# Four edits to a Mamba and attention encoder step: another order of PSUM banks, an earlier split of one weight tile, moved transposes, and a state update in fp32r

## The chip, the cores and the metric

The kernel runs on one core of a Trainium2 chip. The metric is the device time of one execution in microseconds; the figure for the kernel before is the median of three runs, 2209.36 us (2208.69 to 2213.75). Every instruction of the program is in the trace of one profiled execution.

## The reference

Two requests go through one network in one step: a prompt of 512 frames and a sample of 32 frames, which share all weights. Both are kept side by side as 544 columns of a matrix with 1024 rows. The layers are, in order:

```
for i in (0, 1):                                   # D_MODEL 1024, D_FF 2816, everything float32
    if i == 1: k_new, v_new = norm(x) @ w_k, norm(x) @ w_v          # 4 heads of 64
    x += 0.5 * swiglu(norm(x))                                       # FFN 2i
    x += mamba2(norm(x)) if i == 0 else stick_breaking_attention(norm(x), k, v)
    x += 0.5 * swiglu(norm(x))                                       # FFN 2i+1
    x += sigmoid(norm(x) @ w_gate) * (p[i] @ w_proj)                 # per-layer inputs
return norm(x), states, new keys and values
```

Mamba's recurrence is evaluated by chunks, 32 heads in 4 groups of 8. For a chunk with its inputs `x_c`, `B_c`, `C_c` and the summed decay `a_cs`:

```
y         = (C_c B_c^T * decay) x_c + (C_c state) * exp(a_cs)
new_state = state * exp(a_cs[-1]) + B_c^T (exp(a_cs[-1] - a_cs) * x_c)       # the state update
```

The new state of each group is 128 x 512 (state size by heads times head size). The outputs include the final states, the new keys and values, and the convolution's last rows.

## The kernel before

**Products.** A float32 product is made from three products of fp32r parts. An operand is split into a high part (`hi`, a copy by ScalarE or GpSimd that rounds to fp32r) and a low part (`lo`, the rest, by a subtraction on VectorE or GpSimd); the sum of `hi*hi`, `hi*lo` and `lo*hi` is gathered in PSUM. Weights arrive by DMA in tiles of 128 x 1024, are split on chip into `whi` and `wlo`, and are used once. A down, gate or input product of 128 rows takes 8 blocks of 3 parts and 2 column halves of 272. A few small products run in plain float32 instead: the transposes, Mamba's per-head products and the state update, which is one matmul of 512 columns.

**Who orders the work.** In FFNs, Mamba and attention the order on TensorE, VectorE, ScalarE and GpSimd is written by a planner (`Plan`, line 67). The work is a set of chains, each of which yields requests: `T`, `S`, `V`, `G` with an estimated time for an instruction on an engine, `get` and `put` for a buffer slot, `wait` and `set` for an event, `spawn` for a new chain with a rank. `run` (line 145) takes the request that can start first by its own model; among those that could start at the same time, the lowest rank goes first. The engines then run their lists strictly in that order. Outside these three stages (the keys and values, the per-layer inputs, the end) the framework orders the instructions.

**FFN** (`Sevens`, line 579). Most of a product is made by seven products of half size instead of eight. The last four hidden blocks of the FFN go into the output as four plain units `("d", 0)` to `("d", 3)`: units 0 and 1 begin and finish output tiles 0 to 3, unit 2 makes tiles 4 and 5, unit 3 tiles 6 and 7. Each finished tile is added to `x` by VectorE (`leave`, rank 9), and then the next layer's operand is made from it (`onward`, rank 2: `xh` or `nh` on ScalarE, `xl` or `nl` on VectorE, a square on ScalarE and `acc` on VectorE). `halve` (line 745, rank 10) splits a weight tile. There are three weight slots (`NW`); one lies in memory that closes with the stage, and the last three units of the list may not use it. In FFN 0 and 2 a tile of the next stage follows unit `("d", 3)` in the list; in FFN 1 and 3 it is the last.

**PSUM of FFN and its neighbours.** `banks` (line 2067) gives four pairs of banks, pair k being banks 2k and 2k+1. A counter goes round them: each `psum()` and each `roles()` moves it by one. `roles()` with the counter at k gives the FFN's roles A, B, D, X the pairs k, k+1, k+3, k+2 modulo 4. The last tiles 4, 5, 6, 7 go into A, B, D, X where the swaps of A and X between the products come out even, as they do in FFN 2 (16 of them). From FFN 1 to FFN 2 one counter, which starts at 2, serves `roles()`, then 17 calls in the per-layer inputs, then the keys, then `roles()` again.

**Keys and values** (`keys`, line 1605). Four products in the order v0, v1, k0, k1, with the norm's scale after the first. Then the two value tiles are transposed in five blocks of rows, each into a `psum()` of its own, copied to SBUF by VectorE, and stored to memory by two DMAs.

**Attention** (line 1633). Its PSUM pool has four tags: `z` (4 banks), `f` (1), `o` (1), `tr` (2). A tag gets its banks when it is first used. The first four query products go into banks in the order of `FIRSTQ`; the first one takes two `z` banks, one for each column half, and works on blocks 0 to 6 of the first half (21 matmuls), then of the second, and then on block 7.

**Mamba** (line 1110). `dense` walks through the list `MSEQ`: `i` is the six input products of a group (B, C and four x), `z` its gates, `o` its outputs; it has the lowest priority. A group's inputs lie in a slot `grp`, of which there are two. `ssd(g)` works through five chunks, four of the prompt and one of the sample (32 rows), and gives `grp` back when the last is out. For each chunk:

- `turn_x` transposes x, scales it (`xd`, VectorE) and weighs it for the state (`xw`, GpSimd).
- `turn_b` transposes B and copies it (`btok`, VectorE).
- `decay` makes `ex` on ScalarE and VectorE; `decay_ab` makes `exp` of the summed decay on ScalarE and multiplies it by C on GpSimd (`ab`, for chunks after the first).
- `state` does the matmul `btok` by `xw` and adds the old state, decayed on GpSimd.
- `output` (which waits for `ex`, `xd`, `xw`, `ab` and the state before) does the heads' products and adds the skip.

Of the kernel before, what the change touches and what calls it, by code (L numbers as in the profile page):

```python
# [9 lines left out]
P = 128  # L10
# [3 lines left out]
TS = 32  # L14
# [168 lines left out]
def v_cost(n):  # L183
    return n / 960.0 + 0.069


def _body(tc, io):
# [22 lines left out]
    with ExitStack() as ctx:  # L210
# [368 lines left out]
        class Sevens:  # L579
# [91 lines left out]
            def weights(self):  # L671
                raw, tmp = self.raw, self.tmp
                for k, u in enumerate(self.units):
# [48 lines left out]
                    if u[0] == "p" and self.opened and u[1] >= LOWER:  # L722
                        yield "spawn", self.lower(k, src, hi, lo, free), 10
                    else:
                        yield "spawn", self.halve(k, n, src, hi, lo, free), -2 if k == 0 and self.opened else 10

            def fourth(self, it):
                yield "wait", ("part", self.index[it, 2])
# [381 lines left out]
        def mamba(norm, after, ready, ahead):  # L1110
            with tc.tile_pool(name="mt", bufs=1, reuse_waits="tile") as tmp, \
# [254 lines left out]
                def decay_ab(g, c, ab):  # L1366
                    off, n = chunks[c]
                    src = off if c < 4 else SOFF
                    ct = got["C", g][:, src:src + n]
                    yield "S", s_cost(8 * n), lambda: S.activation(ab, ab, AF.Exp), "exp"  # L1370
                    yield "get", "fade"
                    fade = got["fade", g, c] = tmp.tile([P, 8, 1], F32, tag="fade", name="fade", bufs=2)
                    yield "V", 0.08, lambda: V.tensor_copy(fade, ab[:, :, n - 1:n])
                    yield "set", ("fade", g, c)
                    if c > 0:
                        yield "G", 0.06 + 8 * n * 2.28e-3, lambda: G.tensor_tensor(out=ab, in0=ab, in1=ct.unsqueeze(1).to_broadcast([P, 8, n]), op=ALU.mult)
                    yield "set", ("cd", g, c)

                def turn_x(g, c):
                    off, n = chunks[c]  # L1380
                    src = off if c < 4 else SOFF
                    xs = got["x", g]
                    yield "get", "xd"
                    yield "get", "aux"
                    px = aux()

                    def turn():
                        for t in range(4):
                            TE.transpose(px[:n, t * P:(t + 1) * P], xs[:, t, src:src + n], ident)
                    yield "T", 0.44, turn  # L1390
                    xd = got["xd", g, c] = tmp.tile([P, 8, 64], F32, tag="xd", name="xd", bufs=2)
                    yield "W", v_cost(512), lambda: V.tensor_tensor(out=xd[:n], in0=px[:n, :].rearrange("p (h d) -> p h d", d=64),
                                                                 in1=tok[:n, c, 32 + 8 * g:40 + 8 * g].unsqueeze(2).to_broadcast([n, 8, 64]), op=ALU.mult)
                    yield "put", "aux"
                    yield "set", ("xd", g, c)
                    yield "get", "xw"
                    xw = got["xw", g, c] = tmp.tile([P, 8, 64], F32, tag="xw", name="xw", bufs=2)
                    yield "G", 1.0, lambda: G.tensor_tensor(out=xw[:n], in0=xd[:n],
                                                             in1=tok[:n, c, 64 + 8 * g:72 + 8 * g].unsqueeze(2).to_broadcast([n, 8, 64]), op=ALU.mult)
                    yield "set", ("xw", g, c)  # L1400

                def turn_b(g, c):
# [3 lines left out]
                    yield "get", "aux"  # L1406
                    pb = aux()
                    yield "T", 0.11, lambda: TE.transpose(pb[:n, :P], got["B", g][:, src:src + n], ident)
                    btok = got["bt", g, c] = tmp.tile([P, P], F32, tag="btok", name="btok", bufs=1)
                    yield "W", v_cost(P), lambda: V.tensor_copy(btok[:n, :], pb[:n, :P])  # L1410
                    yield "put", "aux"
                    yield "set", ("bt", g, c)

# [10 lines left out]
                def state(g, c):  # L1424
# [4 lines left out]
                    yield "T", 0.87, lambda: TE.matmul(pst, got["bt", g, c][:n, :], got["xw", g, c][:n].rearrange("p h d -> p (h d)"), start=True, stop=True)  # L1429
                    yield "put", "xw"  # L1430
                    yield "put", "btok"
                    if c > 0:
# [23 lines left out]
                def output(g, c):  # L1456
                    off, n = chunks[c]
                    src = off if c < 4 else SOFF
                    xs = got["x", g]
                    need = [("ex", g, c), ("xd", g, c), ("xw", g, c), ("cd", g, c)]  # L1460
                    yield "wait", *need
                    if c > 0:
                        yield "wait", ("st", g, before(c))
# [141 lines left out]
        def keys(norm, psum, tmp, ring, kept, side):  # L1605
# [3 lines left out]
            for which in (1, 0):  # L1609
                for a in range(2):  # L1610
# [7 lines left out]
                    nc.scalar.dma_start(io["kv_out"][which, a], t)  # L1618
                    if which:
                        vT[a] = t  # L1620
                    else:
                        nc.gpsimd.dma_start(kept[0][:, a, :], t)
            vt = side.tile([P, 5, 256], F32, name="vtok")
            for blk in range(5):
                n = P if blk < 4 else TS
                ps = psum()
                for a in range(2):
                    TE.transpose(ps[:n, 0, a * P:(a + 1) * P], vT[a][:, blk * P:blk * P + n], ident)
                V.tensor_copy(vt[:n, blk, :], ps[:n, 0, :256])
            nc.gpsimd.dma_start(kept[1], vt[:, 0:4, :])  # L1630
            nc.gpsimd.dma_start(kept[2], vt[:TS, 4, :])

        def attention(norm, after, ready, ahead, kept):
            with ExitStack() as keep, \
# [11 lines left out]

                def bank(tag):
                    return pp.tile([P, 512], F32, tag=tag, name=tag, bufs=BANKS[tag])

                def two(tag="z"):  # L1650
                    return [bank(tag), bank(tag)]
# [674 lines left out]
```

## Time and profile before

| what | value |
|---|---|
| median of three runs | 2209.36 us |
| profiled execution, its own time | 2208.82 us |
| its span, first to last instruction | 2207.0 us |
| TensorE clock granted, mean | 0.998 |
| busy: TensorE, VectorE, ScalarE, GpSimd | 99%, 81%, 52%, 28% |

The span is what the trace covers; 1.82 us of the profiled execution lie around it. All instructions that go through the kernel's helper class carry its line, L199, so groups are told apart by the names of their tiles. In a timeline a row is: start in us, length in us, engine, line, operation, output<-inputs, shape, count, and in brackets the idle time before it and what ended that. The length of a matmul's row runs past the start of the next, since matmuls are pipelined and their ends are modelled: what a matmul costs is read from the starts of the rows.

### The profile page before, as it was taken

To read this page: it belongs to the slowest core of one execution; us is meant where nothing else is said; L and a number is where in the kernel's file an instruction comes from. 1 tells how busy PE (TensorE), PEld (TensorE's weight loads), DVE (VectorE), ACT (ScalarE), POOL (GpSimd) and SP (SyncE) were. 2 spreads that over 40 slices of the span, in tenths; PEclk is the share of its full clock that TensorE was granted. 3 is DMA by queue.
4 is the path that set the end of the run, shared out by engine and by line. 5 is a ranking of instruction groups with operands and counts; after the bars stand their busy time and mean duration, and the time that the engine had idled before them with its cause. 6 is when DMAs were issued, how large, how long until landed. Compare 5 with 4: busy or idle time off the path is not lost.

```text
span 2207.0 us, 42789 instructions
## 1 busy us (share of the span) xinstructions
PE 2182.7 (99%) x17480; PEld 2128.4 (96%) x17480; DVE 1788.0 (81%) x2460; ACT 1136.8 (52%) x1645; POOL 616.6 (28%) x610
## 2 busy tenths in 40 slices
PE   9999999999999999999999999999999999999998
PEld 9999999999999999999999999999987899999997
DVE  8988887678887689888867798888778799888866
ACT  6444534567756465445355554444456364445354
POOL 1323321254333123223210222322243223233202
PEclk9999999999999999999999999999999999999999
DMA  7686852333333276968532768685411186868422
GB/s 234 158 226 158 213 141 71 113 113 93 111 109 90 91 194 165 229 167 206 145 95 87 222 172 225 167 211 139 126 39 58 49 223 165 222 166 210 129 87 80
DMA packets 119684, 325.53 MB, mean 147 GB/s; under 512 B 15392, under 2 KB 36512, under 8 KB 119488
## 3 DMA queue, kind: packets, MB, share of 16 engines
q1 hardware_dynamic: 92192, 234.81, 32.8%
q0 software_dynamic: 24416, 82.46, 21.0%
q10 hardware_dynamic: 2880, 5.53, 0.7%
q8 instruction: 138, 2.26, 0.4%
q14 instruction: 58, 0.48, 0.1%
HBM read 316.04 MB, written 6.71 MB: 146 GB/s over the span
## 4 chain that ended last, share of the span: by engine, by line
PE 90%; DVE 5%; DMA 2%; ACT 1%; issue 1%; POOL 0%; DVEq 0%; SPq 0%; ACTq 0%; POOLq 0%
PE mm L199 79%; PE z L199 4%; PE aux L199 3%; DMA a<-in_wd 2%; PE f L199 1%; DVE wlo L199 1%; DVE x L199 1%; PE tr L199 1%; PE o L199 1%; DVE xl L199 1%; DVE s L199 1%; DMA plr<-in_p 0%; ACT xh L199 0%; DVE gu L199 0%; DVE nl L199 0%
## 5 line engine op out<-in xcount | busy, mean ns | idle before, releaser
L199 PE MATMUL mm<-xh,whi 128*128 128x272 f32 x1728 | 421.6, 293 | 1.9 <-DVE rm L199 0.9
L199 PE MATMUL mm<-xl,whi 128*128 128x272 f32 x1728 | 414.1, 288 | 0.3 <-DVE xl L199 0.3
L199 PE MATMUL mm<-xh,wlo 128*128 128x272 f32 x1728 | 413.2, 288 | 0.0
L199 PEld LDWEIGHTS mm<-xh,whi 128*128 128x128 f32 x1728 | 293.0, 188 | 11.8 <-issue 9.7
L199 PEld LDWEIGHTS mm<-xl,whi 128*128 128x128 f32 x1728 | 292.5, 188 | 0.5 <-DVE xl L199 0.5
L199 PEld LDWEIGHTS mm<-xh,wlo 128*128 128x128 f32 x1728 | 292.8, 188 | 0.0
L199 PE MATMUL mm<-xfh,whi 128*128 128x272 f32 x936 | 270.0, 288 | 0.0
L199 PE MATMUL mm<-xfh,wlo 128*128 128x272 f32 x936 | 269.9, 288 | 0.0
L199 PE MATMUL mm<-xfl,whi 128*128 128x272 f32 x936 | 269.7, 288 | 0.0
L199 DVE TENSOR_TENSOR wlo<-wraw,whi 128x1024 fp32r<-128x1024 f32 (+3 forms) x179 | 219.9, 1230 | 52.4 <-ACT whi L199 43.1
L199 ACT ACTIVATE whi<-wraw 128x1024 fp32r<-128x1024 f32 (+3 forms) x145 | 147.5, 1020 | 194.6 <-PE mm L199 137.8
L199 ACT ACTIVATE whi<-s 128x1024 fp32r<-128x1024 f32 (+1 forms) x126 | 122.2, 970 | 207.1 <-PE mm L199 99.7
L199 ACT ACTIVATE whi<-a 128x1024 fp32r<-128x1024 f32 (+1 forms) x127 | 125.4, 987 | 159.4 <-PE mm L199 107.9
L199 DVE TENSOR_TENSOR wlo<-a,whi 128x1024 fp32r<-128x1024 f32 (+1 forms) x146 | 168.4, 1154 | 30.7 <-ACT whi L199 25.9
L199 PE MATMUL mm<-h4h,whi 128*128 128x272 f32 x688 | 178.2, 289 | 3.4 <-DVE x L199 3.4
L199 PE MATMUL mm<-h4h,wlo 128*128 128x272 f32 x688 | 177.7, 289 | 1.2 <-DVE wlo L199 1.2
L199 PE MATMUL mm<-h4l,whi 128*128 128x272 f32 x688 | 177.4, 288 | 0.0
L199 PEld LDWEIGHTS mm<-xfl,whi 128*128 128x128 f32 x936 | 176.1, 188 | 0.0
L199 PEld LDWEIGHTS mm<-xfh,wlo 128*128 128x128 f32 x936 | 176.1, 188 | 0.0
L199 PEld LDWEIGHTS mm<-xfh,whi 128*128 128x128 f32 x936 | 176.0, 188 | 0.0
L199 DVE SCALAR_TENSOR_TENSOR x<-mm,x 128x544 f32<-128x544 f32 x200 | 143.8, 719 | 37.4 <-PE mm L199 37.0
L199 DVE TENSOR_TENSOR wlo<-s,whi 128x1024 fp32r<-128x1024 f32 (+1 forms) x136 | 154.8, 1138 | 21.2 <-ACT whi L199 13.3
(378 smaller groups left out, 6027.5 us busy)
## 6 DMA issues: line engine op xcount, KB each, us to landing
a<-in_wgq SPq DMA_DIRECT2D x117, 512.0 KB, 5.7
s<-in_wgq POOLq DMA_DIRECT2D x79, 512.0 KB, 7.0
a<-in_wd SPq DMA_DIRECT2D x72, 384.0 KB, 4.3
wraw<-in_win SPq DMA_DIRECT2D x41, 512.0 KB, 3.6
s<-in_wgq SPq DMA_DIRECT2D x40, 512.0 KB, 4.7
wraw<-in_wgq SPq DMA_DIRECT2D x38, 512.0 KB, 5.0
wraw<-in_wgq POOLq DMA_DIRECT2D x38, 512.0 KB, 8.3
s<-in_wd SPq DMA_DIRECT2D x24, 384.0 KB, 4.8
```

What stands on the lines that cost most here:

```text
L199: ins = getattr(self.engine, op)(*args, **kw)
```

## The change

It has four parts.

1. **Attention's banks.** A loop at the start of attention uses each tag once, so that `o` gets its bank first, then the four of `z`, then `f` and `tr`.
2. **Last down tiles.** The split of unit `("d", 3)` runs at rank 8 instead of 10, in all four FFNs.
3. **Values.** The transposes stand between the products k0 and k1. The first four blocks share one `psum()` and one copy of 128 x 1024; the fifth has its own. Three fewer `psum()` calls are made.
4. **Mamba's state update.** `xw` and the transposed B are split into fp32r parts, and the product is made from three matmuls. The high part of `xw` is a copy on ScalarE, the low part a subtraction on VectorE; B's high part is read from PSUM by ScalarE, its low part by VectorE, where the copy was. `output` waits for the new event `xr`, which is set before the split. The multiplication of `ab` by C goes from GpSimd to VectorE.

```diff
 (Sevens.weights)
-                        yield "spawn", self.halve(k, n, src, hi, lo, free), -2 if k == 0 and self.opened else 10
+                        yield "spawn", self.halve(k, n, src, hi, lo, free), -2 if k == 0 and self.opened else 8 if u[0] == "d" and u[1] == 3 else 10
 (decay_ab)
-                        yield "G", 0.06 + 8 * n * 2.28e-3, lambda: G.tensor_tensor(out=ab, in0=ab, ...)
+                        yield "V", v_cost(8 * n), lambda: V.tensor_tensor(out=ab, in0=ab, ...)
 (turn_x)
                     yield "G", 1.0, lambda: G.tensor_tensor(out=xw[:n], in0=xd[:n], ...)
+                    yield "set", ("xr", g, c)
+                    flat = xw[:n].rearrange("p h d -> p (h d)")
+                    high = tmp.tile([P, 512], F32R, tag="xwh", name="xwh", bufs=2)
+                    yield "S", s_cost(512), lambda: S.activation(high[:n, :], flat, AF.Copy)
+                    low = tmp.tile([P, 512], F32R, tag="xwl", name="xwl", bufs=2)
+                    yield "V", v_cost(512), lambda: V.tensor_tensor(out=low[:n, :], in0=flat, in1=high[:n, :].bitcast(F32), op=ALU.subtract)
+                    got["xw", g, c] = high, low
                     yield "set", ("xw", g, c)
 (turn_b)
-                    btok = got["bt", g, c] = tmp.tile([P, P], F32, tag="btok", name="btok", bufs=1)
-                    yield "W", v_cost(P), lambda: V.tensor_copy(btok[:n, :], pb[:n, :P])
+                    high = tmp.tile([P, P], F32R, tag="btok", name="btok", bufs=1)
+                    yield "S", s_cost(P, True), lambda: S.activation(high[:n, :], pb[:n, :P], AF.Copy)
+                    low = tmp.tile([P, P], F32R, tag="btol", name="btol", bufs=1)
+                    yield "W", v_cost(P), lambda: V.tensor_tensor(out=low[:n, :], in0=pb[:n, :P], in1=high[:n, :].bitcast(F32), op=ALU.subtract)
+                    got["bt", g, c] = high, low
 (state)
-                    yield "T", 0.87, lambda: TE.matmul(pst, got["bt", g, c][:n, :], got["xw", g, c][:n]..., start=True, stop=True)
+                    def products():
+                        (bh, bl), (wh, wl) = got["bt", g, c], got["xw", g, c]
+                        for k, (b, w) in enumerate(((bh, wh), (bh, wl), (bl, wh))):
+                            TE.matmul(pst, b[:n, :], w[:n, :], start=k == 0, stop=k == 2)
+                    yield "T", 0.7, products
 (output)
-                    need = [("ex", g, c), ("xd", g, c), ("xw", g, c), ("cd", g, c)]
+                    need = [("ex", g, c), ("xd", g, c), ("xr", g, c), ("cd", g, c)]
 (keys)
-                    else:
-                        nc.gpsimd.dma_start(kept[0][:, a, :], t)
-            vt = side.tile([P, 5, 256], F32, name="vtok")
-            for blk in range(5):
-                n = P if blk < 4 else TS
-                ps = psum()
-                for a in range(2):
-                    TE.transpose(ps[:n, 0, a * P:(a + 1) * P], vT[a][:, blk * P:blk * P + n], ident)
-                V.tensor_copy(vt[:n, blk, :], ps[:n, 0, :256])
-            nc.gpsimd.dma_start(kept[1], vt[:, 0:4, :])
-            nc.gpsimd.dma_start(kept[2], vt[:TS, 4, :])
+                        continue
+                    nc.gpsimd.dma_start(kept[0][:, a, :], t)
+                    if a:
+                        continue
+                    vt = side.tile([P, 5, 256], F32, name="vtok")
+                    for blks in (range(4), range(4, 5)):
+                        n = P if blks[0] < 4 else TS
+                        ps = psum()
+                        for k, blk in enumerate(blks):
+                            for b in range(2):
+                                at = 256 * (k % 2) + b * P
+                                TE.transpose(ps[:n, k // 2, at:at + P], vT[b][:, blk * P:blk * P + n], ident)
+                        V.tensor_copy(vt[:n, blks[0]:blks[-1] + 1, :]..., ps[:n, :, :]...[:, :256 * len(blks)])
+                    nc.gpsimd.dma_start(kept[1], vt[:, 0:4, :])
+                    nc.gpsimd.dma_start(kept[2], vt[:TS, 4, :])
 (attention)
+                for tag in ("o", "z", "z", "z", "z", "f", "tr", "tr"):
+                    bank(tag)
```

More of the change, by code (lines that the diff above doesn't have):

```diff
@@ L1375, in decay_ab @@
                     if c > 0:
-                        yield "G", 0.06 + 8 * n * 2.28e-3, lambda: G.tensor_tensor(out=ab, in0=ab, in1=ct.unsqueeze(1).to_broadcast([P, 8, n]), op=ALU.mult)
+                        yield "V", v_cost(8 * n), lambda: V.tensor_tensor(out=ab, in0=ab, in1=ct.unsqueeze(1).to_broadcast([P, 8, n]), op=ALU.mult)
                     yield "set", ("cd", g, c)
@@ L1396, in turn_x @@
                     yield "get", "xw"
-                    xw = got["xw", g, c] = tmp.tile([P, 8, 64], F32, tag="xw", name="xw", bufs=2)
+                    xw = tmp.tile([P, 8, 64], F32, tag="xw", name="xw", bufs=2)
                     yield "G", 1.0, lambda: G.tensor_tensor(out=xw[:n], in0=xd[:n],
                                                              in1=tok[:n, c, 64 + 8 * g:72 + 8 * g].unsqueeze(2).to_broadcast([n, 8, 64]), op=ALU.mult)
+                    yield "set", ("xr", g, c)
[5 more added lines that the diff above has]
+                    got["xw", g, c] = high, low
                     yield "set", ("xw", g, c)
@@ L1428, in state @@
                     pst = aux()
-                    yield "T", 0.87, lambda: TE.matmul(pst, got["bt", g, c][:n, :], got["xw", g, c][:n].rearrange("p h d -> p (h d)"), start=True, stop=True)
+                    def products():
[3 more added lines that the diff above has]
+                    yield "T", 0.7, products
                     yield "put", "xw"
@@ L1620, in keys @@
                         vT[a] = t
-                    else:
-                        nc.gpsimd.dma_start(kept[0][:, a, :], t)
-            vt = side.tile([P, 5, 256], F32, name="vtok")
-            for blk in range(5):
-                n = P if blk < 4 else TS
-                ps = psum()
-                for a in range(2):
-                    TE.transpose(ps[:n, 0, a * P:(a + 1) * P], vT[a][:, blk * P:blk * P + n], ident)
-                V.tensor_copy(vt[:n, blk, :], ps[:n, 0, :256])
-            nc.gpsimd.dma_start(kept[1], vt[:, 0:4, :])
-            nc.gpsimd.dma_start(kept[2], vt[:TS, 4, :])
+                        continue
[10 more added lines that the diff above has]
+                                TE.transpose(ps[:n, k // 2, at:at + P], vT[b][:, blk * P:blk * P + n], ident)
+                        V.tensor_copy(vt[:n, blks[0]:blks[-1] + 1, :].rearrange("p k n -> p (k n)"), ps[:n, :, :].rearrange("p a n -> p (a n)")[:, :256 * len(blks)])
+                    nc.gpsimd.dma_start(kept[1], vt[:, 0:4, :])
+                    nc.gpsimd.dma_start(kept[2], vt[:TS, 4, :])
         def attention(norm, after, ready, ahead, kept):
```

## The prediction

> **What bounds the kernel now.** I read the page's busy shares first, then its chain of work that ended last.
>
> ```profile
> span 2207.0 us, 42789 instructions
> ...
> PE 2182.7 (99%) x17480; PEld 2128.4 (96%) x17480; DVE 1788.0 (81%) x2460; ACT 1136.8 (52%) x1645; POOL 616.6 (28%) x610
> ...
> PE 90%; DVE 5%; DMA 2%; ACT 1%; issue 1%; POOL 0%; DVEq 0%; SPq 0%; ACTq 0%; POOLq 0%
> ```
>
> TensorE (PE) is busy all but 24.3 us of the span, so time can only be won in two ways: by giving PE less to do, or by closing one of its few gaps. Next come two stretches in the view of busy times, an FFN's and the part of Mamba in which the scan runs. The columns are the stretch, its length, and the busy time of PE, weight loads, DVE, ACT and POOL.
>
> ```profile
> 28.00:366.00 338.00, 336.93 (x2682) 336.14 (x2681) 286.58 (x362) 155.17 (x203) 92.68 (x86) 1.00 0.66 168
> 425.00:720.00 295.00, 294.10 (x2531) 275.11 (x2530) 228.73 (x420) 199.45 (x341) 111.62 (x129) 1.00 0.35 105
> ```
>
> Mamba's PE stands idle for only 0.9 of 295 us, with DVE at 78%; the FFN's PE is idle for 1.1 us with DVE at 85%. So in Mamba it is PE's own work that counts, and 85% of DVE is a load that this kind of order has borne. Last, PE's waits, by what ended them (total us, times, longest):
>
> ```profile
> PE mm L199 <- DVE wlo L199: 1.2, 2, 0.7
> PE z L199 <- DVE x L199: 1.2, 1, 1.2
> ...
> PE mm L199 <- DVE kv L199: 0.7, 1, 0.7
> ```
>
> These four gaps are what parts 1 to 3 of the change touch. What they cost PE is read from the starts of matmuls below, since a row's length runs past the next start.
>
> **The state update: less PE work.** Two stretches of PE's timeline, around a product of 128 rows and around one of the sample's 32:
>
> ```profile
> 429.92 1.02 PE L199 MATMUL aux<-xw,btok 128*128 128x512 f32 x2
> 430.37 0.81 PE L199 MATMUL mm<-xh,whi 128*128 128x272 f32 x2
> 431.02 0.41 PE L199 MATMUL mm<-xl,whi 128*128 128x272 f32 x2
> 431.27 0.41 PE L199 MATMUL mm<-xh,wlo 128*128 128x272 f32 x2
> ...
> 486.41 1.12 PE L199 MATMUL aux<-xw,btok 32*128 32x512 f32 x2
> ...
> 487.82 0.41 PE L199 MATMUL mm<-xl,whi 128*128 128x272 f32 x2
> ```
>
> A pair of fp32r matmuls of 272 columns takes 0.25 us (431.02 to 431.27), 0.125 each. From 429.92 to 431.02 lie the state product and one such pair, so the product costs 1.10 - 0.25 = 0.85 us. With 32 rows it is 1.41 - 0.25 = 1.16, of which 0.31 must be changes of shape. There are 16 of the first (four groups, four prompt chunks) and 4 of the second. An fp32r matmul of 512 columns is in the trace among attention's logits, two at a time on 64 rows each:
>
> ```profile
> 1617.57 0.40 PE L199 MATMUL z<-kl,qq 64*128 64x512 f32 x2
> 1617.81 0.39 PE L199 MATMUL z<-kh,qq 64*128 64x512 f32 x2
> ```
>
> That is 0.24 us for 512 columns; scaling 0.125 by 512/272 gives 0.235. I take 0.235, so three cost 0.705, and I let the 0.31 of the sample's shape stay. Saved: 16 x (0.85 - 0.705) = 2.3, and 4 x (1.16 - 0.705 - 0.31) = 0.6, together **2.9 us**. Bounds: 2.1 if a matmul costs 0.24 and the sample saves nothing; 5.4 if it costs 0.85/4 = 0.213 and the 0.31 goes too.
>
> **What the state update adds elsewhere.** Durations by group:
>
> ```profile
> L199 POOL TENSOR_TENSOR ab<-ab,C 128x1024 f32<-128x1024 f32 x12 | 28.7, 2392 | 30.9 <-DVE fade L199 30.9
> L199 DVE TENSOR_TENSOR ex<-ex,cb 128x1024 f32<-128x1024 f32 x16 | 19.6, 1227 | 3.5 <-ACT ex L199 3.5
> ...
> L199 DVE TENSOR_TENSOR qq<-qT,qq 128x512 fp32r<-128x512 f32 x7 | 5.6, 800 | 2.3 <-ACT qq L199 2.3
> L199 ACT ACTIVATE qq<-qT 128x512 fp32r<-128x512 f32 x6 | 3.8, 626 | 3.6 <-DVE qT L199 3.6
> ```
>
> The `ab` multiplication leaves POOL. On DVE it should take what `ex` by `cb` of the same shape takes, 1.23 us: 12 x 1.23, and some 2 us for the four of the sample, make 16.4 us. The low part of `xw` adds 20 x 0.80 = 16.0 at most, and B's low part takes the copy's place at about the same cost. DVE's load in the scan goes from 228.7 to about 261 of 295 us, 88%. ACT gets 20 x 0.63 for `xw` and some 5 us for B: about 17 on 199. All of this lies beside PE work. The split of `xw` delays only `state`, since `output` waits for `xr`; and `output`, which needs `ab`, gets it 2.39 - 1.23 = 1.16 us earlier for each chunk when DVE is free. The planner writes all of Mamba's lists anew from the changed costs. The cover that could go is the room between a group's last output and the input product that wants its `grp` slot. I put +0.2 us on the new order, with bounds from -0.9 (every idle moment closed) to +12.7 (below).
>
> **The last down tile.** DVE's, POOL's and PE's timelines near the end of FFN 1, then PE's at the end of FFN 3:
>
> ```profile
> 1133.19 1.16 POOL L199 TENSOR_SCALAR whi<-wraw 128x1024 fp32r<-128x1024 f32 x1 [8.58 <-PE mm L199]
> ...
> 1136.21 1.54 DVE L199 TENSOR_TENSOR acc<-acc,sq 128x544 f32<-128x544 f32 x2
> 1138.37 0.72 DVE L199 SCALAR_TENSOR_TENSOR x<-mm,x 128x544 f32<-128x544 f32 x1
> 1139.01 1.22 DVE L199 TENSOR_TENSOR wlo<-wraw,whi 128x1024 fp32r<-128x1024 f32 x1
> ...
> 1139.38 0.41 PE L199 MATMUL mm<-h4l,whi 128*128 128x272 f32 x2
> 1140.28 0.52 PE L199 MATMUL mm<-h4h,wlo 128*128 128x272 f32 x2 [0.48 <-DVE wlo L199]
> ```
>
> ```profile
> 2125.00 0.41 PE L199 MATMUL mm<-h4l,whi 128*128 128x272 f32 x2
> 2126.09 0.52 PE L199 MATMUL mm<-h4h,wlo 128*128 128x272 f32 x2 [0.68 <-DVE wlo L199]
> ```
>
> The high part is there at 1134.35, but DVE does the subtraction only at 1139.01, behind tile additions (rank 9) and the next norm's work (rank 2). PE could have gone on at 1139.63 and starts at 1140.28: 0.65 lost; in FFN 3, 2126.09 - 2125.25 = 0.84. At rank 8 the subtraction passes the additions, though not the rank 2 work. It needs only be done by 1139.63, and moving ahead of the addition at 1138.37 and one more is enough. The additions then come up to 1.14 us later; their next readers are PE's bank for tiles 6 and 7 and the per-layer gates, both microseconds away. FFN 0 and 2 show no wait for this tile. I take **1.4** of 1.49; bounds 0 and 1.49.
>
> **The values.** PE and DVE at the end of the keys' stage:
>
> ```profile
> 1231.72 0.82 PE L199 MATMUL mm<-ident,kv 128*128 128x128 f32 x6
> 1233.26 0.72 PE L199 MATMUL mm<-ident,kv 128*128 128x128 f32 x4 [0.72 <-DVE kv L199]
> 1234.02 0.49 PE L199 MATMUL mm<-xh,whi 128*128 128x272 f32 x2
> ...
> 1229.70 2.87 DVE L199 SCALAR_TENSOR_TENSOR xl<-x,gains,xh 128x544 fp32r<-128x544 f32 x4 [1.73 <-ACT xh L199]
> 1232.49 0.72 DVE L199 TENSOR_TENSOR kv<-mm,r 128x544 f32<-128x544 f32 x1
> ```
>
> Six transposes take 0.66 us (four of them 0.44 to 0.5), so the seventh could start at 1232.38 and starts at 1233.26. The fourth block's PSUM is the pair that k1 just filled, and DVE reads that out only after four `xl`. Moved ahead of k1, the ten transposes cost PE the same, but find v0's and the scale's pairs long free: **0.9 us** saved. What is late next: FFN 2's first operand. Its `xl` move with k1, about 1.1 us later, so blocks 0 to 3 are done by 1233.7 with PE starting near 1233.1 and taking 0.75 per block: enough. The five copies leave the end of the stage; their replacement, one of 128 x 1024, falls into k1's six microseconds, and the two stores on POOL's queue go earlier, past k1's own. Bounds 0 and 1.0.
>
> **Attention's banks.** PE and DVE where FFN 2 ends:
>
> ```profile
> 1589.16 0.41 PE L199 MATMUL mm<-h4h,wlo 128*128 128x272 f32 x2
> 1590.72 0.36 PE L199 MATMUL z<-xh,whi 128*128 128x272 f32 x1 [1.15 <-DVE x L199]
> ...
> 1589.85 0.72 DVE L199 SCALAR_TENSOR_TENSOR x<-mm,x 128x544 f32<-128x544 f32 x1
> ...
> 1592.09 0.72 DVE L199 TENSOR_TENSOR acc<-acc,sq 128x544 f32<-128x544 f32 x1
> ...
> 1594.58 1.08 PE L199 MATMUL tr<-acc,nones 128*128 128x272 f32 x4
> ```
>
> The first query product could start at 1589.41 and starts at 1590.72, when tile 7 has been read out (1589.85 + 0.72): 1.31 lost. Counting calls: FFN 2's `roles()` comes at 2 + 1 + 17 + 10 = 30, so A, B, D, X are pairs 2, 3, 1, 0 and tile 7 lies in banks 0 and 1, where `z` begins. The keys now make three calls fewer: at 27 the roles are pairs 3, 0, 2, 1. Tile 7 is in banks 2 and 3, tile 5 in 0 and 1. With `o` on bank 0, the first `z` is bank 1, tile 5's, free some 6 us before. Should the second `z` be tile 7's, it is wanted 21 x 0.125 = 2.6 us later, when the readout is over. Late next is the norm's sum: `acc` ends at 1592.81 and is wanted at 1594.58 - 1.31 = 1593.27, so 0.46 remains. I take **1.2** of 1.31; bounds 0 and 1.31.
>
> **The sum.** -2.9 + 0.2 - 1.4 - 0.9 - 1.2 = -6.2 on the profiled execution's 2208.82 (span 2207.0 and 1.8 around it): 2202.6. The median before lies 0.5 above its profiled execution; with the same offset the forecast is **2203.1 us**.
>
> **Rivals.**
>
> *Cheaper columns (2201.8).* If an fp32r matmul costs a quarter of the float32 product, 0.213, the state saves 16 x 0.21 + 4 x 0.21 = 4.2 instead of 2.9. For it: the trace's 0.125 may hold a fixed part that does not grow with the columns. Against: the logits' 0.24. [...]
>
> *A late group (2205.9).* The scan of group 0 ends, and the input product that takes its `grp` slot follows, on DVE's timeline:
>
> ```profile
> 492.27 0.25 DVE L199 SCALAR_TENSOR_TENSOR y<-xs,vecs,aux 128x32 f32<-128x32 f32 x1
> ...
> 499.16 0.85 DVE L199 TENSOR_TENSOR cu<-mm,r 128x272 f32<-128x272 f32 x3
> ```
>
> That product takes 48 x 0.125 = 6.0 us up to 499.1, so it began near 493.0, only 0.5 us after the last output at 492.5. If the five chunks' new steps (0.63 on ACT, 0.68 to 0.80 on DVE) come half into their path, that is 3.3 us, and PE stands for 2.8. For it: a list in strict order, and DVE fuller by a tenth. Against: `ab` gets shorter in the same path.
>
> *DVE sets Mamba's pace (2215.6, slower than before).* From 475 to 600 us DVE has most to do. If the additions there, 32.4 x 125/295 = 13.7 less 1.0 of waiting that shrinks, hide behind nothing, since the scan's reads of PSUM, the dense products' evictions and the weight splits all stand in DVE's one list, PE loses 12.7 in place of 0.2. It decides from 6.4 us of lost PE time on. For it: 88% as a mean over the scan is more than the FFN's 85%. Against: about 15 us of DVE's time in that stretch stay free. [...]
>
> *Two edits without effect (2205.7).* Rank 2 work keeps the subtraction back, and `z` still begins on a bank that is read out late: 1.4 + 1.2 not won. For it: ranks decide only among requests that could start at once. Against: the count of calls above.
>
> **Chances.** Forecast 0.50, with its own range 2201.7 to 2204.8; cheaper columns 0.14; a late group 0.18; two edits without effect 0.10; DVE's pace 0.08. The range 2200.0 to 2209.0 holds all but the last and part of the tails. This kernel's measurement tells about 0.3%, 6.6 us, from no change, so faster means below 2202.7: 0.4 of the forecast's chance, nearly all of cheaper columns, and a little of the others, 0.38. Slower means above 2216.0: about half of the last case, and the tails, 0.05. The rest, 0.57, is the same within 0.3%.
>
> **What the new profile should show.** Three fp32r matmuls of 512 columns for each chunk, spaced 0.21 to 0.24; no wait of PE for `wlo` at the ends of FFN 1 and 3; the transposes between k0 and k1, with no wait for `kv`; attention's first `z` matmul right behind the last down tile; PE idle under 2 us in 425 to 720. I am wrong if PE shows new waits for `cu`, `xs` or `ex` in Mamba that add up to more than 2 us, or if any of the three gaps stands in its old place.

## The result, and the profile after

The changed kernel takes 2205.66 us (median of 20 runs, 2201.33 to 2211.22), the kernel before 2209.89 (20 runs): a ratio of 0.9978, with a 95% interval of 0.9971 to 0.9986, so 3.1 to 6.4 us less. The forecast was 2203.1, in a range of 2200 to 2209. The profiled execution of the changed kernel took 2208.17 us and stands 2.5 us above its own median, so its span says little; what follows is read from its stages.

The busy shares on the page of the changed kernel:

```profile
PE 2181.4 (99%) x17500; PEld 2133.3 (97%) x17500; DVE 1813.4 (82%) x2496; ACT 1143.7 (52%) x1677; POOL 582.7 (26%) x599
```

The stretch of the busy times in which Mamba's scan runs, as before (length; then PE, weight loads, DVE, ACT, POOL):

```profile
425.00:720.00 295.00, 292.77 (x2546) 280.92 (x2545) 249.75 (x448) 209.35 (x374) 83.44 (x118) 1.00 0.35 105
```

In the scan DVE has gone from 228.7 to 249.8 us and POOL from 111.6 to 83.4. DVE was forecast at 261: the low part of `xw` took 0.69 us and not 0.80, and over Mamba the rows of `wlo` and `cv` came out 4.4 us shorter in all; the rest was not broken down. But PE now stands idle for 2.2 of 295 us instead of 0.9. PE's waits over the whole kernel (total, times, longest):

```profile
PE mm L199 <- DVE x L199: 5.0, 11, 0.8
...
PE mm L199 <- ACT xh L199: 1.4, 1, 1.4
PE mm L199 <- DVE cu L199: 1.3, 1, 1.3
...
PE mm L199 <- DVE wlo L199: 1.2, 3, 0.5
```

`z <- x` (1.2 us) and `kv` (0.7) are gone, and so is `acc` (0.8), which the prediction did not speak of. New are 1.3 us for `cu` and 1.3 more for `x`. The three waits for `wlo` are not those of before: they stand at 992, 1533 and 1977 us, well inside FFN 1, 2 and 3, and none is left at the ends of FFN 1 and 3.

To see where time was won, I laid PE's matmuls of both executions side by side wherever they come in the same order, and read how far the changed kernel is ahead. The places at which that jumps: 0.89 us at the entry to Mamba (`acc`), 1.31 across Mamba, 0.65 and 0.69 at the last down tiles of FFN 1 and 3, of which 0.43 and 0.48 are lost again 8 us later, 1.14 from the gates to the end of the keys' stage, and 1.31 at attention's start. That is 5.1 us in all. Other jumps, of both signs, are for the most part waits for work that hangs on the arrival of weights, and in this pair of executions they take 4.6 us back, so that the spans differ by only 0.5. They differ from one execution to the next: the wait for `xh` at 7 to 8 us, for one, is 0.5 us in the one profile and 1.4 in the other, where the clock then stands at 0.50 for 3.4 us (8.2 to 11.6). What the change is worth is therefore read from the medians and from the places above, not from the two spans.

**The state products.** PE around the first chunk's and the first sample's products:

```profile
430.74 0.40 PE L199 MATMUL aux<-xwh,btok 128*128 128x512 f32 x1
430.97 0.40 PE L199 MATMUL aux<-xwl,btok 128*128 128x512 f32 x1
431.21 0.39 PE L199 MATMUL aux<-xwh,btol 128*128 128x512 f32 x1
431.44 0.41 PE L199 MATMUL mm<-xh,whi 128*128 128x272 f32 x2
...
478.23 0.49 PE L199 MATMUL aux<-xwh,btok 32*128 32x512 f32 x1
478.56 0.39 PE L199 MATMUL aux<-xwl,btok 32*128 32x512 f32 x1
478.80 0.38 PE L199 MATMUL aux<-xwh,btol 32*128 32x512 f32 x1
479.12 0.52 PE L199 MATMUL mm<-xh,whi 128*128 128x272 f32 x2
```

Three products take 431.44 - 430.74 = 0.70 us, 0.233 each; the sum had 0.705.

**The two new waits in Mamba.** DVE's list ahead of the longer one, and PE at its end:

```profile
629.89 0.67 DVE L199 TENSOR_TENSOR st<-st,aux 128x512 f32<-128x512 f32 x1
631.44 1.23 DVE L199 TENSOR_TENSOR wlo<-wraw,whi 128x1024 fp32r<-128x1024 f32 x1 [0.88 <-ACT whi L199]
...
632.84 0.85 DVE L199 TENSOR_TENSOR cu<-mm,r 128x272 f32<-128x272 f32 x3
```

```profile
633.83 0.49 PE L199 MATMUL mm<-xh,whi 128*128 128x272 f32 x2 [1.32 <-DVE cu L199]
```

PE wants a bank that `cu` has to read out; the last matmul of that product started by 630.3. `cu` stands in DVE's list behind a weight split whose high part ACT has not finished, and so DVE idles for 0.88 us with the work that PE needs next in hand. The shorter wait, 0.8 us for `x` at 567.50, also has DVE late with a readout: of the two slots for dense products one has been full since 562.7, and DVE reads it (`zt`) only at 568.05, so that PE has to wait for the other.

**The last down tile.** DVE and PE at the end of FFN 1:

```profile
1138.54 1.22 DVE L199 TENSOR_TENSOR wlo<-wraw,whi 128x1024 fp32r<-128x1024 f32 x1
...
1146.90 0.72 DVE L199 SCALAR_TENSOR_TENSOR x<-mm,x 128x544 f32<-128x544 f32 x1
```

```profile
1139.96 0.42 PE L199 MATMUL mm<-h4h,wlo 128*128 128x272 f32 x2
...
1147.67 0.52 PE L199 MATMUL mm<-plh,whi 128*128 128x272 f32 x2 [0.28 <-DVE x L199]
```

The subtraction ends at 1139.76 and PE goes on at 1139.96 without a wait. A gate product then waits for the last of the additions. In the kernel before, that addition is

```profile
1146.82 0.72 DVE L199 SCALAR_TENSOR_TENSOR x<-mm,x 128x544 f32<-128x544 f32 x1
```

It ends at 1147.54 before and at 1147.62 after (2133.34 and 2133.23 behind FFN 3). So it has hardly moved: DVE does the same work ahead of it in another order, with next to no idle time. It is PE that comes 0.65 us earlier and has to wait.

**Values and banks.** PE in the keys' stage, then at attention's start, and DVE there:

```profile
1225.78 1.25 PE L199 MATMUL mm<-ident,kv 128*128 128x128 f32 x10
1226.79 0.50 PE L199 MATMUL mm<-xh,whi 128*128 128x272 f32 x2
```

```profile
1589.55 0.41 PE L199 MATMUL mm<-h4h,wlo 128*128 128x272 f32 x2
1589.80 0.29 PE L199 MATMUL z<-xh,whi 128*128 128x272 f32 x1
```

```profile
1590.25 0.72 DVE L199 SCALAR_TENSOR_TENSOR x<-mm,x 128x544 f32<-128x544 f32 x1
```

Ten transposes run as one row of 1.0 us, and the first `z` follows the last down tile after 0.25 us, although tile 7's addition ends only at 1590.97.

### The profile page after: what moved, and what is told of

Read it like the earlier page. It is cut to its first block, busy times and chain, and to the rows that moved or that the text cites. A ratio compares the mean times of both kernels' runs of the same rounds, so it can differ in the third digit from the quotient of the medians.

```text
span 2206.5 us, 42864 instructions
## 1 busy us (share of the span) xinstructions
PE 2181.4 (99%) x17500; PEld 2133.3 (97%) x17500; DVE 1813.4 (82%) x2496; ACT 1143.7 (52%) x1677; POOL 582.7 (26%) x599
## 4 chain that ended last, share of the span: by engine, by line
PE 91%; DVE 4%; DMA 2%; ACT 1%; issue 1%; POOL 0%; DVEq 0%; SPq 0%; POOLq 0%; ACTq 0%
PE mm L199 80%; PE z L199 4%; PE aux L199 3%; DMA a<-in_wd 2%; PE f L199 1%; PE tr L199 1%; DVE wlo L199 1%; PE o L199 1%; DVE x L199 1%; DVE s L199 0%; DVE nl L199 0%; DMA plr<-in_p 0%; DVE xl L199 0%; DVE gu L199 0%; DVE acc L199 0%
## 5 line engine op out<-in xcount | busy, mean ns | idle before, releaser
L199 PE MATMUL mm<-xh,whi 128*128 128x272 f32 x1728 | 417.0, 290 | 3.7 <-ACT xh L199 1.4
L199 ACT ACTIVATE whi<-wraw 128x1024 fp32r<-128x1024 f32 (+3 forms) x138 | 140.1, 1018 | 163.8 <-PE mm L199 118.1
L199 DVE TENSOR_TENSOR wlo<-s,whi 128x1024 fp32r<-128x1024 f32 (+1 forms) x136 | 155.0, 1140 | 26.8 <-ACT whi L199 19.6
```

The lines of the kernel that those rows point to most:

```text
L199: ins = getattr(self.engine, op)(*args, **kw)
```

## The experiments

Mamba is measured from PE's first product of the norm's sum to its first product in FFN 1 that reads `h4h`. Its two ends in the changed kernel:

```profile
372.09 0.47 PE L199 MATMUL aux<-acc,nones 128*128 128x272 f32 x1
...
797.37 0.41 PE L199 MATMUL mm<-h4h,nones 128*128 128x272 f32 x2
```

| kernel | Mamba, us | waits of PE in its scan, us | time of the kernel, us | kernel before, in the same session, us |
|---|---|---|---|---|
| before | 426.59 | 0.9 | 2209.89 | 2209.89 |
| changed | 425.27 | 2.1 | 2205.66 | 2209.89 |
| e1, state update alone | 425.31 | 2.1 | 2210.93 | 2211.38 |
| e2, the same, ab on GpSimd | 442.19 | 14.1 | 2228.39 | 2211.38 |
| e3, ab on VectorE alone | 439.31 | 7.7 | 2222.81 | 2211.38 |
| e8, changed, other list | 422.57 | 0 | 2203.35 | 2210.92 |
| e9, changed, a third list | 433.34 | 7.6 | 2217.36 (one run) | 2211.93 |
| e10, e3 with another list | 425.11 | 0 | 2209.43 (one run) | 2211.93 |
| e11, e2 with another list | 426.37 | 2.2 | 2210.37 (one run) | 2211.93 |
| e12, e8 without the banks' lines | 422.58 | 0 | 2202.75 | 2211.93 |

The kernel before came out up to 2 us apart in the four sessions, so a time is to be compared with its neighbour in the last column. e4 to e7 were run once each: 2210.91 us (before: 2211.38), then 2209.99, 2211.38 and 2207.59 (before: 2210.92); what they show is read from their traces.

**State update alone (e1).** The six edits in Mamba, nothing else:

```diff
-  yield "G", ..., lambda: G.tensor_tensor(out=ab, in0=ab, in1=ct..., op=ALU.mult)
+  yield "V", v_cost(8 * n), lambda: V.tensor_tensor(out=ab, in0=ab, in1=ct..., op=ALU.mult)
...
-  yield "T", 0.87, lambda: TE.matmul(pst, ...)
+  yield "T", 0.7, products
```

> The kernel before with the state update's edits alone (fp32r products, split of xw and B, ab on VectorE). Mamba is measured on PE from the first product of its norm's sum to the dense matmul that stands at 736.60 us before and at 734.60 in the changed kernel: 363.8 us before, 362.5 in the changed kernel. Theory 1, the planner's new lists: this stage depends on no other edit, so it takes 362.5 again, the two waits of 1.3 us (cu) and 0.8 us (x) stand in the same places, and the whole kernel is 1.3 us faster than before. Rival, the waits come from the other edits or from one disturbed execution: they are missing here, and the stage takes 363.8 - 3.1 - 1.2 = 359.5 us, the whole kernel 4.3 us less.

This expectation and the next two end the stage earlier, at a matmul that stands at 736.60 us before; the difference between two kernels is what can be compared. The stage took 425.31 us, with 0.8 us for `x` at 569 and 1.3 for `cu` at 635, as in the changed kernel. So these waits belong to this part of the change and are no accident of one execution. By time the kernel is not to be told from the one before: 0.9997 (0.9989 to 1.0006), which holds the expected -1.3 us.

**ab on GpSimd (e2), and ab's move alone (e3).** e2 leaves out the first pair of lines above; e3 consists of them only.

> The same edits, but the multiplication of ab by C stays on GpSimd. Theory 1, any rewriting of the lists brings waits of this size somewhere: the stage takes 361.5 to 363, with waits of PE of 1 to 2.4 us in all, in other places. Theory 2, ab on VectorE is what makes VectorE late for cu and x, by its own 12 x 1.2 us and by shutting GpSimd's instructions out: no wait over 0.3 us is left in the stage, GpSimd's copies take 1.05 us and not 2.1, and the stage takes 359.5 to 360.7 us, 3 to 4 us less than before. Rival, GpSimd is what the edit relieves: ab is late for the outputs, and the stage is longer than 362.5.

> The kernel before, with only the multiplication of ab by C moved from GpSimd to VectorE; the products stay float32. Theory 2 (ab makes VectorE late): the stage grows from 363.8 by 1 to 2.4 us, and waits for cu or x of 0.8 us and more appear. Theory 1: the stage stays within 0.6 us of 363.8. Rival, the move is a gain of its own since outputs get ab 1.16 us earlier: the stage shrinks by the waits of before, 1.2 us, to 362.6.

Both are misses: every theory that gave a size had it wrong. e2 lost 15.6 us in the stage and the kernel 0.73% (0.60 to 0.85), e3 12.7 us and 0.56% (0.43 to 0.70). Some of PE's waits in e2, then the longest in e3:

```profile
PE mm L199 <- DVE cu L199: 3.7, 1, 3.7
PE aux L199 <- ACT xwh L199: 2.6, 1, 2.6
PE aux L199 <- POOL ab L199: 2.5, 2, 2.0
```

```profile
PE aux L199 <- POOL xw L199: 5.6, 1, 5.6
```

The rival that GpSimd is what the move relieves fits e2, where PE waits for POOL's `ab` and for what stands behind it. But e3, with POOL relieved and the products as before, should then have won, and lost almost as much. POOL and DVE in e3 show how:

```profile
485.24 3.81 POOL L199 TENSOR_SCALAR cstate<-cu 128x3 f32<-128x3 f32 x2
489.02 1.57 POOL L199 TENSOR_TENSOR xw<-xd,tok 32x512 f32<-32x512 f32 x1
```

```profile
485.76 1.20 DVE L199 TENSOR_TENSOR wlo<-wraw,whi 128x1024 fp32r<-128x1024 f32 x1
...
487.79 1.20 DVE L199 TENSOR_TENSOR ab<-ab,C 128x1024 f32<-128x1024 f32 x1
```

Two copies of 128 x 3, of which 19 of the 48 in that list take 0.25 us or less, took 3.81: the first ended when DVE's `wlo` did (487.0 us), the second when its `ab` did (489.0). Why the second was not done in the 0.8 us before `ab` began is not shown. The last `xw` of the group stands behind them, and behind that PE. Whether this belongs to ab on VectorE or to the one order in which the planner put it is what e10 was for.

The waits in e3 add up to 7.7 us, 6.8 more than before, and the stage lost 12.7. The rest is in the clock. Three stretches of e3 behind the wait, with the granted clock third from the end of each row:

```profile
490.30:497.10 6.80, 6.45 (x38) 4.62 (x39) 2.33 (x5) 5.26 (x12) 0.29 (x1) 0.50 0.10 38
497.12:500.50 3.38, 1.30 (x21) 0.90 (x19) 2.44 (x8) 0.09 (x1) 1.67 (x1) 1.00 0.57 155
500.55:507.30 6.75, 6.62 (x39) 5.43 (x36) 4.52 (x12) 4.23 (x11) 1.04 (x1) 0.50 0.40 119
```

At the end of the wait of 5.6 us the clock falls to half for 6.8 us. It falls once more, for another 6.8 us, after a stretch in which PE waited 0.7 and 1.4 us and was busy for 1.3 of 3.4. PE's 13.1 us of work at half the clock cost some 6.5 us, against the 5.9 that the waits leave open. A wait can thus be paid for twice; behind the changed kernel's wait of 1.3 us the clock stays at 1.00:

```profile
633.80:637.00 3.20, 3.17 (x24) 3.05 (x24) 3.20 (x11) 2.48 (x5) 1.11 (x5) 1.00 0.98 291
```

**Another list for the same work (e8, e9, e10, e11).** One number of the planner's model, the cost that it takes for a chunk's state products, is changed. What is computed stays the same. The greedy planner writes another order, and because it also chooses the engine of some weight splits, copies and additions, a few instructions change engine as well: in e8 five weight splits go from GpSimd to ScalarE and three other instructions to GpSimd, in e10 against e3 one copy goes from GpSimd to ScalarE. The expectations below, which speak of the order alone, missed that.

```diff
-                    yield "T", 0.7, products
+                    yield "T", 0.8, products     # e8;  0.79 in e9;  0.74 in e11;  float32: 0.87 -> 0.95 in e10
```

> The changed kernel with one number of the planner's changed, the cost that it takes for a chunk's three state products (0.8 us in place of 0.7). Every instruction stays, only their order in the four engines' lists of Mamba is another. Theory 1, what Mamba loses is a matter of the list: the stage (PE's first product of the norm's sum to FFN 1's first combined product, 425.3 us in the changed kernel, 426.6 before) moves by 1 us or more, with the waits of 1.3 and 0.8 us gone and others in their place; if the waits add up to under 1 us, the stage takes 423 to 424 and the kernel is 1 to 2.5 us faster than the changed one. Theory 3, VectorE's load sets the loss: the load is the same, so the waits add up to 2 us again and the stage takes 425.3 with 0.5 to either side.

> The changed kernel with the planner's cost of a chunk's state products at 0.79 us in place of 0.7: again only the order in Mamba's four lists is another. Theory 1 (the list): neighbouring costs can give lists that differ by many us, so PE has waits of 2 us and more in all in Mamba's scan, unlike the run with 0.8 (422.6 us and no wait over 0.1 us), and the stage lies above 425. Theory 3 (the load of the engines sets the stage): between 422 and 426 us as with the costs 0.7 and 0.8.

> The kernel before with only ab's multiplication on VectorE, as in the earlier run of 439.3 us, and the planner's cost of the float32 state product at 0.95 us in place of 0.87. Theory 1: the 12.7 us that ab's move cost there belong to that one list; with another the stage takes 425 to 427 us, waits under 1 us in all, and GpSimd's xw is not held up for 5 us. If there are no waits, the stage lies above the 422.6 of fp32r products without waits by what the products cost more, 20 x 0.16 = 3.2: 425.8. Rival, ab on VectorE is what starves GpSimd: a wait for xw of 3 us or more stands again and the stage is over 430.

> The state update by fp32r products with ab's multiplication left on GpSimd, as in the earlier run of 442.2 us, and the planner's cost of the products at 0.74 us. Theory 1: another list takes most of the 15.6 us back; the stage takes 424 to 429 us. Theory 2', with ab on GpSimd the splits of xw come too late for any list (xw stands behind a 2.4 us ab on GpSimd): waits for xwh, xwl or ab of 5 us and more are left, and the stage takes 432 us or more.

The stretch from 425 to 720 us in e8, then in e9:

```profile
425.00:720.00 295.00, 295.00 (x2583) 282.57 (x2582) 251.30 (x454) 215.75 (x381) 86.31 (x117) 1.00 0.35 106
```

```profile
425.00:720.00 295.00, 287.41 (x2462) 275.57 (x2462) 243.74 (x435) 208.28 (x364) 86.48 (x114) 0.99 0.35 106
```

In e8 PE stands idle for nothing in 295 us, with DVE at 251.3, as full as in any of these kernels. So VectorE's load is not what the changed kernel loses by. The stage came out just under the 423 to 424 us that were expected without waits. The kernel takes 2203.35 us, 0.9966 (0.9954 to 0.9978) of the one before: it beats both, by 2.7 us of Mamba and some 2 us of time, though the intervals of the two ratios still touch. e9 stands 0.01 us away in that one number and 10.8 us away in the stage: theory 1, with a wider spread than it asked for. Order and engine choice are not separated there; between e3 and e10, with one copy moved, it is almost the order alone. PE's longest waits in e9:

```profile
PE aux L199 <- DVE ab L199: 3.0, 2, 1.7
PE aux L199 <- DVE xd L199: 2.9, 2, 2.5
```

The lengths can be accounted for. Against the lists without waits (e8, and for e3 e10) the stage is longer by 19.6 us in e2, 14.2 in e3, 10.8 in e9 and 3.8 in e11; the waits (14.1, 7.7, 7.6 and 2.2) and half of the time that PE worked at half its clock (5.6, 6.5, 3.2 and 1.7) add up to 19.7, 14.2, 10.8 and 3.9. In e11 it is a wait of only 2.0 us for `xwh`, with one of 0.2 behind it, that the lowered clock follows:

```profile
572.30:575.60 3.30, 3.30 (x16) 3.30 (x16) 1.71 (x5) 0.95 (x3) 0.89 (x2) 0.50 0.16 47
```

e10 took 425.11 and e11 426.37: 14.2 of e3's 439.31 and 15.8 of e2's 442.19 went with the list alone. So neither place of `ab` costs those 12 to 16 us, and nothing here shows that moving it to VectorE is a gain by itself; e11 keeps a 2.0 us wait for `xwh`, and whether a list without it exists was not tried. e10 against e8, both without a wait, is the price of float32 against fp32r products: 425.11 - 422.57 = 2.5 us, where their spacing said 3.2. The entries into products of another shape, about 0.1 us each (0.33 and 0.32 us where the sample's products begin and end in the rows above, 0.24 between), stand at other places in the two lists and may be the rest; that was not separated.

**The last down tile's rank alone (e4).**

```diff
-  ..., -2 if k == 0 and self.opened else 10
+  ..., -2 if k == 0 and self.opened else 8 if u[0] == "d" and u[1] == 3 else 10
```

> The kernel before with only the last down tile's rank 8 in place of 10. Theory 1, the subtraction goes ahead of the tile additions and these are then late for the gates: PE's waits for wlo (0.65 us at 1139.5 and 0.84 at 2125.1) are gone, and a wait of PE for x of 0.4 to 0.5 us appears behind each, 6 to 8 us later, in the gate products; the net gain is 0.4 to 0.6 us of 1.49. Rival, the one of the prediction: the additions have room, the gate waits of the changed kernel come from something else in it, and here only the gain of 1.4 shows.

PE in the gate products behind FFN 1, and at the entry to Mamba:

```profile
1149.76 0.52 PE L199 MATMUL mm<-plh,whi 128*128 128x272 f32 x2 [0.31 <-DVE x L199]
```

```profile
374.98 1.16 PE L199 MATMUL aux<-acc,nones 128*128 128x272 f32 x4
```

The gates' wait is there without the rest of the change: 0.47 us behind FFN 1 and 0.47 behind FFN 3 in place of 0.65 and 0.84. But a third wait is gone as well. In the kernel before, this row is

```profile
372.78 0.47 PE L199 MATMUL aux<-acc,nones 128*128 128x272 f32 x1 [0.77 <-DVE acc L199]
```

It stands with 0.77 us in all eight kernels that keep rank 10 (before, e1, e2, e3, e5, e6, e10, e11), and not at all in the five with rank 8 and the subtraction on VectorE. In FFN 0 no matmul waited for the subtraction. What held up the norm's sum there was one `acc`, an addition of two operands in SBUF, beside a weight split on POOL. Both in the kernel before, then that `acc` in e4:

```profile
362.07 1.09 POOL L199 TENSOR_SCALAR whi<-wraw 128x1024 fp32r<-128x1024 f32 x1 [4.95 <-PE mm L199]
...
362.16 1.57 DVE L199 TENSOR_TENSOR acc<-acc,sq 128x544 f32<-128x544 f32 x1
```

```profile
364.66 0.72 DVE L199 TENSOR_TENSOR acc<-acc,sq 128x544 f32<-128x544 f32 x1
```

`acc` takes 0.72 us alone and 1.57 here. DVE's list has next to no idle time from there to the norm's sum, so these 0.85 us reach PE's first product in Mamba. With rank 8 one addition to `x` comes later and `acc` begins 0.5 us before POOL's split; two additions, which read one operand (`mm`) from PSUM, stand beside it and take no longer than elsewhere (in the changed kernel, whose list has the same two there, 1.34 us for both beside the split, as 1.35 for two in e7 with no POOL work beside them). All eight kernels with the wait have an `acc` of 1.56 or 1.57 us at this place, and the five without it have 0.71 or 0.72.

**The subtraction on GpSimd (e7).** The changed kernel, with

```diff
+  if self.units[k][0] == "d" and self.units[k][1] == 3:
+      yield "G", 0.05 + n * 2.3e-3, lambda: G.tensor_tensor(out=lo[:, :n], in0=src[:, :n], ..., op=ALU.subtract)
+  else:
       yield self.either(...)
```

> The changed kernel, with the subtraction of the last down tile on GpSimd, which has nothing else to do there, in place of VectorE. Theory, what is late is VectorE, which has 1.2 us too much in the last 12 us of an FFN: with the subtraction gone from it both waits are gone, PE's for wlo and the one for x of 0.43 and 0.48 us in the gate products of FFN 1 and 3, so 0.9 us less in all. Rival, GpSimd's subtraction of 2.4 us and VectorE's instructions with two inputs from SBUF shut each other out: VectorE's instructions of 0.7 us beside it grow to 2 us or more, the additions are late all the same and the waits for x stay at 0.4 us or grow.

POOL and DVE at the end of FFN 1, then PE in the gate products:

```profile
1134.93 2.75 POOL L199 TENSOR_TENSOR wlo<-wraw,whi 128x1024 fp32r<-128x1024 f32 x1
```

```profile
1133.15 0.78 DVE L199 SCALAR_TENSOR_TENSOR nl<-x,gains,nh 128x544 fp32r<-128x544 f32 x1
...
1134.48 3.79 DVE L199 SCALAR_TENSOR_TENSOR nl<-x,gains,nh 128x544 fp32r<-128x544 f32 x2
```

```profile
1146.71 0.52 PE L199 MATMUL mm<-plh,wlo 128*128 128x272 f32 x2 [0.29 <-DVE wlo L199]
```

The rival came true in its mechanism. Two `nl`, 0.78 us each alone, took 3.79 beside POOL's 2.75: the second ends 0.6 us behind POOL's subtraction. Taking 1.2 us from DVE cost it 2.2. In the gate products PE now waits for `wlo` of the gates' weights, 0.45 us behind FFN 1 and 0.54 behind FFN 3, and still 0.31 and 0.32 for `x`. The wait for `acc` came back with 1.8 us; an `acc` in FFN 0 takes 2.28 us beside POOL's subtraction.

**Banks alone (e5), values alone (e6), all but the banks (e12).**

```diff
+                for tag in ("o", "z", "z", "z", "z", "f", "tr", "tr"):     # e5 alone; left out in e6 and e12
+                    bank(tag)
```

> The kernel before with only the three lines that take attention's banks in another order. Theory, the count of calls: without the keys' edit roles() still comes at 30, tile 7 of FFN 2 lies in banks 0 and 1, and the first z moves from bank 0 to bank 1, which is read out as late. PE's wait for x where attention begins stays at 1.2 to 1.35 us, and the kernel's time stays what it was. Rival, the order of the banks is what wins the 1.3 us: the wait is under 0.3 us.

> The kernel before with only the keys' and values' edit. Theory, the count of calls: roles() comes at 27, tile 7 lies in banks 2 and 3 and tile 5 in 0 and 1, so attention's first z on bank 0 is free early; the wait of 1.3 us at attention's start is gone without the new order of the banks, and the wait for kv of 0.86 us at the end of the keys is gone too; from the gate products to attention's first z PE takes 2.0 to 2.4 us less than the 444.8 of before, waits in FFN 2 apart. Rival, both edits are needed: the first z still falls on a bank that is read out late, and the 1.3 us stay.

> The changed kernel with the planner's cost at 0.8 and without the three lines that order attention's banks. Count of calls: the keys' edit alone already moves tile 7 away from the first z, so no wait over 0.3 us stands at attention's start, attention takes the same time, and the kernel takes what the one with cost 0.8 took, 2203 us with 1.5 to either side, 0.3 to 0.4% less than before. Rival, the order of the banks is worth its 1.3 us beside the keys' edit: the wait stands again and the kernel takes 2204.5 or more.

Attention's first `z` in e5, and in e6:

```profile
1593.11 0.36 PE L199 MATMUL z<-xh,whi 128*128 128x272 f32 x1 [1.15 <-DVE x L199]
```

```profile
1592.92 0.41 PE L199 MATMUL mm<-h4h,wlo 128*128 128x272 f32 x2
1593.18 0.29 PE L199 MATMUL z<-xh,whi 128*128 128x272 f32 x1
```

The order of the banks alone leaves the wait as it was, and the keys' edit alone takes it away; over all traces the wait stands in the eight kernels without that edit and in none of the six with it. In e6 the way from the gates to attention was not the 2.0 to 2.4 us shorter as it stands (445.2 against 444.8 us): waits of FFN 2 on arriving weights and on `x` came to 3.9 us there, against 1.25 before; without these it is 2.3 shorter. e12, the changed kernel with e8's list and without the banks' lines, has no wait at attention's start and takes 2202.75 us, 0.996 (0.9946 to 0.9973) of the kernel before: as fast as e8.

## Why the prediction was right, and where it was not

The time lies in the range, and 2.6 us above the forecast. The total came out of terms of which some were wrong in opposite ways.

- **The state products: right.** 0.705 us was taken for three, 0.70 was measured, and the cheaper columns (0.213, the author's guess of a quarter of the float32 product) did not come: 0.233. Between lists without waits the saving is 2.5 us, against 2.9.
- **Mamba's new order: the term that failed, by its size.** +0.2 was put on it; the stage won 1.3 instead of 2.9, so it was +1.6, or +1.2 if the saving is the 2.5 measured between lists without waits; that 1.2 is what PE's waits in the scan grew by, from 0.9 to 2.1 us. The mechanism, a strict list in which a readout stands behind something late, was named among the rivals, but at the `grp` slot of group 0, where no wait came. A bound was derived from DVE's load, and e8 shows that load has little to do with it: the same work has lists of 422.6, 425.3 and 433.3 us. The 15 us of DVE's time that the prediction left free from 475 to 600 us do not follow from its rows either (105.0 busy of 125, and 13.7 more, leave 6); 15.8 were free, since DVE grew by less. PE's idle time in the scan, 2.2 us, missed the "under 2" of its signs. The right statement ahead of time would have been that the order is drawn anew and is worth -2.7 to +8.1 us (e8 and e9 against the changed kernel).
- **The last down tile: the gain right, the cover wrong.** Of 1.49 us 1.34 was won, but "both microseconds away" was wrong for the gates: they gave back 0.43 and 0.48 (0.47 twice in e4). The prediction asked how late the additions may come, and not how early PE would then want the last of them, which stays where it was. "FFN 0 and 2 show no wait for this tile" was true; the 0.89 won at FFN 0's end came from `acc` no longer standing beside a POOL split, which nobody had planned. Net 1.3, near the 1.4 by luck.
- **The values: right.** 0.9 forecast, 1.1 measured, and what was late next, FFN 2's first operand, shows no wait in the changed kernel.
- **The banks: right in the count, wrong in the credit.** The 1.31 us went as forecast (1.2). But it is the keys' three calls fewer that move tile 7; the new order of the banks is without effect in every kernel tried (e5, e6, e12). The prediction's own count said so, had it asked which bank the old order would begin on at 27: bank 0, tile 5's.
- **The rivals.** DVE setting Mamba's pace is ruled out by e8. Of two edits without effect one is: the banks' lines.

With the 1.3 that Mamba won in place of 2.7, the prediction's sum would have been -4.8 us, against -4.2 measured.

## What to carry to other kernels

Where a greedy planner writes engine lists, an edit of its work is worth its direct saving plus a new draw of the order, and here the draw (-3 to +8 us) was larger than the saving (2.5 us); so an edit that looks bad in one list is not yet bad, and several lists should be tried by changing a modelled cost. When an instruction is moved ahead on a full engine, the last result of that engine stays where it was, and whoever needs it will wait for it instead; look also at what the other engine then runs beside its instructions: here an `acc` took 1.57 us beside a POOL split and 0.72 without. Count which rotating buffer each consumer gets before and after: an edit that only changes the number of calls can do what another edit was written for.

## What the runs showed of the hardware

Instructions of VectorE and GpSimd that ran beside each other took longer in these rows, in both directions: DVE's `nl` took some 2.9 us beside a POOL subtraction and 0.78 without (e7), its `acc` 1.57 beside a POOL split and 0.72 without (before), and POOL's 128 x 3 copies 1.8 and 2.1 us beside DVE's `wlo` and `ab`, where others took under 0.2 (e3). The copies ended within 0.1 us of `wlo` and `ab`, and `acc` and `nl` 0.6 us behind POOL's instruction. I had expected the first; new was that a copy of three elements per partition was held up for longer than either DVE instruction lasted (1.2 us), and twice in a row.

The clock fell to 0.50 after PE had waited for 5.6 us (e3), which the sum of no part had allowed for. It also fell after shorter waits: in e11 after 2.0 and 0.2 us, with PE busy for 1.25 of the 3.4 us before; in e8's FFN 1 after 1.2 and 0.5 us, with PE busy for 1.64 of 3.35; in e3 the second time after 0.7 and 1.4 us, with PE busy for 1.3 of 3.4; and in the changed kernel at 8.2 us after 1.4 us, with PE busy for 2.0 of 3.4. The changed kernel's wait of 1.3 us for `cu` passed at 1.00. What decides between these is not shown.

In the changed kernel POOL was still held up: at 623.52 a weight split beside DVE's `ex` times `cb` took 2.10 us, twice its 1.05.
